# Weight pieces from one planned list, source order in the feed-forwards, and transposes of both token tiles

## The chip, the core and the metric

The kernel runs on one core of a Trainium2 chip. The metric is device time in microseconds (us) of one execution; the median of several runs counts, less is better.

## The reference

One decoder layer on 256 tokens of width 2048, all in float32:

```
x = x + 0.5 * swiglu(rmsnorm(x, w1), ffn1)        # gate, up: 2048 x 5632, down: 5632 x 2048
x = x + mixer(rmsnorm(x, w2))                     # w_in: 2048 x 8208, w_out: 2048 x 2048
x = x + 0.5 * swiglu(rmsnorm(x, w3), ffn2)
out = rmsnorm(x, w4)
swiglu(x) = (silu(x @ w_gate) * (x @ w_up)) @ w_down
```

The mixer has 8 heads of retention (rotary positions, fixed decays, a row norm and a gate) and 8 heads of a gated delta rule (a causal convolution over 4 tokens, l2 norms, decays computed from the input, a triangular solve in each chunk, a row norm and a gate). Both read one product with w_in, and one product with w_out takes both.

## The kernel before, in words

**Products.** Tokens stand in NT = 2 tiles of 128. Every weight is read once, in pieces of two row tiles by 512 columns, 512 KB each. A piece is loaded (`raw`, issued by SP, L126) and split exactly in two parts: ScalarE casts it to the high part (`whi`, L130), VectorE subtracts that from it for the low part (`wlo`, L131). The left operand has two parts as well (`xh` and `xl`, or `hh` and `hl`). `triple` (L139) adds three matmuls of 128x128 by 128x512: high by high (L144), high by low (L145), low by high (L146). A unit is one `triple`; a piece is four units, 12 matmuls, and serves both token tiles. `raw`, `whi` and `wlo` have four buffers each, so the cast of piece n + 4 waits until TensorE is done with piece n, and the load of piece n + 4 until VectorE has made `wlo` of piece n.

**Feed-forward** (`ffn`, L278). The 5632 inner columns are 11 blocks of 512, done in two halves of 6 and 5 blocks. A block is the product with w_gate, its silu on ScalarE (`sg`, L311), the product with w_up, and `h` on VectorE (L315): 192 matmuls in 16 pieces. `h` has tokens in the partitions and must become a left operand: VectorE transposes it in squares of 32x32 (`vector_transposed`, L217). One operation takes 32 partitions of one token tile into one quadrant of 32 partitions of `ht`, 32x128 elements; 32 of them make a block. Then ScalarE copies `ht` to `hh` (L136) and VectorE makes `hl` (L137), in two halves. This work is not issued at once: it goes as small functions into the list `later`, and `product` (L207) takes one of them after every second unit of the next product. After a half's blocks come four column blocks of the product with w_down, added to x by VectorE (L331). In the second half of the first feed-forward, x's new columns are transposed and scaled for the mixer's norm in the same way (`norm_block`, L250). The last column block of the last product runs one token tile after the other at its end (`staggered_product`, L174).

**Start.** The first block of the first feed-forward alternates between the two products, two contraction tiles at a time. `start` (L347) loads x transposed, scales it for the first norm (`norm_tile`, L231, on ScalarE and VectorE), loads x itself and sums its squares on ScalarE.

**Mixer** (L423). 16 products with w_in run as units; after each unit, chains of stages (generators) are advanced: convolution, delta rule, retention, rotary angles, and the transposes of the heads' outputs (`mixed_chain`, L830). A stage yields the number of units to wait for. In the delta rule the rows of a matrix go to DRAM and come back broadcast over 32 partitions (`nr`, L721, issued by POOL), and VectorE uses them in `yn` (L736). Two loads of retention's decays (`rd`, L877) are issued from ScalarE's queue.

**What sets the order.** The kernel is written in a framework that follows dependences and buffers by itself. Its scheduler plays the program through with modelled durations and gives each engine a fixed list of instructions: among those that are ready by its model, the one that stands first in the source. Each engine then works through its list in that order, and each instruction waits until what it needs is really there. So an instruction can stand ahead of another one because the model thought that it would be ready sooner.

Of the kernel before, what the change touches and what calls it, by code (L numbers as in the profile page):

```python
# [29 lines left out]
Q = 32           # partitions of a quadrant  # L30
KEPT = 4         # weight pieces of the last product that stay on chip
NLEV = 7         # log2 of the delta-rule chunk (128)
# [11 lines left out]
# columns of the constant table  # L44
# [10 lines left out]
def _constants():  # L55
    """Masks, identity, rotary frequencies and retention decays: functions of shapes alone."""
# [27 lines left out]
def hybrid_layer(ctx: ExitStack, tc: tile.TileContext, a: dict, out: bass.AP):  # L84
    nc = tc.nc
    V, S, G, PE = nc.vector, nc.scalar, nc.gpsimd, nc.tensor

# [12 lines left out]
    # the norms' weights; x transposed follows them  # L100
# [10 lines left out]
    # the tensor engine's clock rises only under load: it starts while the first loads are on their way  # L111
# [6 lines left out]
    # the left operand of every product, as contraction tiles in two parts  # L118
# [4 lines left out]
    def weight_piece(src, k, n, pool=wsp, both=None):  # L123
        """both: where the parts go, instead of tiles of the pool."""
        raw = wraw.tile([P, k, n], F32, name="raw")
        nc.sync.dma_start(raw, src)  # L126
        if both is None:
            both = pool.tile([P, k, n], F32R, name="whi"), pool.tile([P, k, n], F32R, name="wlo")
        hi, lo = both
        S.copy(hi, raw)  # L130
        V.tensor_tensor(lo, raw, hi.bitcast(F32), ALU.subtract)  # L131
        return hi, lo

    def split(hi, lo, src):
# [13 lines left out]
    def product_pieces(rows, w, c0, sizes=()):  # L148
        """The row tiles of w[:, c0:c0+NB] in pieces: (positions in rows, source)."""
# [6 lines left out]

    def product_units(left, w, rows, c0, sizes=()):
        """PSUM accumulators, one per token tile, of left.T @ w[rows, c0:c0+NB], and a generator that fills them.

        left(k): the two parts of contraction tile k, [128, T] each;  # L160
        rows: pairs (k, row tile of w), in order."""
        accs = [acc.tile([P, NB], F32, name="acc") for _ in range(NT)]

        def units():
            for ks, src in product_pieces(rows, w, c0, sizes):
                hi, lo = weight_piece(src, len(ks), NB)
                for j, k in enumerate(ks):
                    for t in range(NT):
                        triple(accs[t], left, rows[k][0], t, hi[:, j, :], lo[:, j, :], k == 0, k == len(rows) - 1)
                        yield  # L170
# [3 lines left out]
    def staggered_product(left, w, rows, c0, pool, kept):  # L174
        """The same product, one token tile after the other at its end; yields an accumulator when it is full.
        The last `kept` pieces of the weight stay in pool."""
# [4 lines left out]
        def piece(i, t):  # L181
            if t == 0:
                ks, src = pieces[i]
                split_pieces[i] = weight_piece(src, len(ks), NB, pool if i >= len(pieces) - kept else wsp)
# [4 lines left out]
        lag = 2  # L189
        for i in range(len(pieces)):  # L190
# [10 lines left out]
    later = deque()      # work whose inputs are on their way: done bit by bit beside the next product  # L201
# [63 lines left out]
    def power(dst, src, e, w):  # L265
        """src ** e, element by element, on a small tile."""
# [11 lines left out]
    def ffn(idx, factor, after, lead=None):  # L278
        """factor(): the row factors; after(b, t, pool): follows the sum of column block b and token tile t;
        lead(k, pool): makes contraction tiles k and k + 1 of the left operand."""  # L280
# [5 lines left out]
        with (tc.tile_pool(name=f"ffn{idx}", bufs=1) as hp, tc.tile_pool(name=f"ffe{idx}", bufs=1) as ep,  # L286
              tc.tile_pool(name=f"wlast{idx}", bufs=KEPT) as wl):
            hh = hp.tile([P, len(halves[0]) * kb, T], F32R, name="hh")
# [5 lines left out]
            for hf in halves:  # L294
                rows = [(k, k) for k in range(KD)]
                for i, b in enumerate(hf):
                    u = None
                    if b == 0 and lead:
                        g, gs = product_units(x_left, wg, rows, 0, (1, 1))
                        u, us = product_units(x_left, wu, rows, 0)  # L300
                        for k in range(0, KD, 2):
                            lead(k, ep)
                            for units in (gs, us):
                                deque(islice(units, 2 * NT), 0)
                    else:
# [18 lines left out]
                for b in range(nout):  # L324
                    if last and idx == 2 and b == nout - 1:
                        o = staggered_product(h_left, wd, rows, b * NB, wl, KEPT)
# [20 lines left out]
    def start(k, pool):  # L347
        """Contraction tiles k and k + 1 from the transposed x; x itself comes along, a column block behind."""
# [28 lines left out]
    ffn(1, lambda: row_factor(ssqs[0]), to_mixer, start)  # L377

# [44 lines left out]
def mixer(tc, a, gd, env):  # L423
# [7 lines left out]
    GH = 4                       # heads of a group  # L431
# [3 lines left out]
    with ExitStack() as ctx:  # L435
# [61 lines left out]
        def gates_chain():  # L497
# [5 lines left out]
            # the weight's two parts side by side as the left operand: their products are added at the end  # L503
# [39 lines left out]
            # exp of sums of g: from the chunk's start to a token, and from a token to the end of chunk 0  # L543
# [8 lines left out]
        def rotary_chain():  # L552
# [15 lines left out]
            # whole turns off, coarsely (any size of position), then the nearest one;  # L568
            # turns and 2 pi in parts whose products are exact
# [38 lines left out]
        def tokens(src, c):  # L608
            """Chunk c of src [channel, 4, tokens] -> PSUM [token, 4, channel]."""
# [22 lines left out]
        def delta_chain(gi, kq, vT):  # L632
            """The delta rule of a group of heads; gates[gi] becomes its gated output."""
            hs = gi * GH
            kT, qT = kq[:, :, 0, :], kq[:, :, 1, :]
            # decays exp(sum of g over (s, t]) of each head and chunk, [s, t], zero for t < s
# [14 lines left out]
            # k and q back to tokens for their norms; k of chunk 0, decayed to the chunk's end  # L651
# [24 lines left out]
            # scores with decay, [s, t]: N.T (its diagonal is never read) and the attention's  # L676
# [13 lines left out]
            # X = (I + N)^-1 and Y = X.T  # L690
# [5 lines left out]
            def quad(f, m=P):  # L696
                """Four narrow products, each beside one of the running product's units, which hide its operand's load."""
# [7 lines left out]
            # blocks of the diagonal of N.T, [row, matrix, column in block], by way of DRAM to all rows of their block  # L705
# [19 lines left out]
            # column j of the inverse's transpose times row j of N.T leaves the columns to the right  # L725
# [18 lines left out]
            # then by doubling the blocks: only the left half of the columns of a doubled block of X changes  # L744
# [26 lines left out]
            # the two chunks  # L771
# [19 lines left out]
            # row norm, with q's own factor in it  # L791
# [57 lines left out]
        def rotated_chain(src, dst):  # L849
            """src [tokens, t, 4*128] -> rotary -> dst [d, 4, tokens]."""  # L850
# [23 lines left out]
        def retention_chain(hs, qT, kT, v, gate):  # L874
            """Retention of a group of heads; the gates, when they come, become its gated output."""
# [123 lines left out]
```

## Time and profile before

Three runs took 2058.64, 2060.18 and 2061.57 us, median 2060.18. The profiled execution has a span of 2058.5 us between its first and last instruction.

| engine | busy us | share of the span | instructions |
|---|---|---|---|
| TensorE, matmuls (PE) | 1995.6 | 97% | 8804 |
| TensorE, weight loads (PEld) | 1617.5 | 79% | 8804 |
| VectorE (DVE) | 1400.9 | 68% | 2390 |
| ScalarE (ACT) | 896.8 | 44% | 1076 |
| GpSimd (POOL) | 89.4 | 4% | 121 |

8160 of the 8804 matmuls are the wide ones of the products. Matmuls are pipelined: one is shown as some 0.39 us long while the next one has started, so a high busy share doesn't say that TensorE is as fast as it can be. The distance between the starts of two matmuls says that. The memory moved 379.94 MB, 185 GB/s over the span; the mean granted clock of TensorE is 0.992 of full speed.

### The profile page before, as it was taken

The numbers are of one execution on the slowest core, as the hardware profiler recorded it, in microseconds if no ns is written. First come the engines' busy times: TensorE is split into PE (matmuls) and PEld (weight loads), VectorE is DVE, ScalarE is ACT, GpSimd is POOL, SyncE is SP. The second block draws the span as 40 slices with busy tenths as digits, with TensorE's granted clock in tenths as the row PEclk, the third lists the DMA queues.
The fourth block names the chain that finished last, engine by engine and source line by source line (L and its number), as shares of the span: only waits on it lengthen the run. The fifth ranks groups of instructions, "written<-read, shape, count | busy, mean of one in ns | idle before, by whom it ended". The sixth has DMA issues, their size and how long they took to land.

```text
span 2058.5 us, 24232 instructions
## 1 busy us (share of the span) xinstructions
PE 1995.6 (97%) x8804; PEld 1617.5 (79%) x8804; DVE 1400.9 (68%) x2390; ACT 896.8 (44%) x1076; POOL 89.4 (4%) x121
## 2 busy tenths in 40 slices
PE   9999999999999999988998989999999999999998
PEld 7777878887787778876877778788887888887786
DVE  6777764457776866564897698866677544677754
ACT  6444443344444446633643334444444434444443
POOL 0000000000000000320132100000000000000000
PEclk9999999999999999999999999999999999999999
DMA  8555655565565565697468545665555656655564
GB/s 302 188 166 184 197 195 189 190 187 171 184 196 196 169 202 174 146 205 172 136 182 190 132 133 195 205 189 188 187 183 173 209 194 192 190 187 164 185 214 143
DMA packets 197608, 379.94 MB, mean 185 GB/s; under 512 B 15280, under 2 KB 15920, under 8 KB 197360
## 3 DMA queue, kind: packets, MB, share of 16 engines
q1 hardware_dynamic: 193600, 367.35, 58.3%
q0 software_dynamic: 3168, 8.65, 1.6%
q10 hardware_dynamic: 720, 2.38, 0.3%
q8 instruction: 69, 1.13, 0.2%
q14 instruction: 51, 0.42, 0.1%
HBM read 375.98 MB, written 2.36 MB: 184 GB/s over the span
## 4 chain that ended last, share of the span: by engine, by line
PE 69%; DVE 22%; DMA 3%; issue 3%; ACT 2%; POOL 1%; SPq 0%; DVEq 0%; POOLq 0%; ACTq 0%
PE acc L145 22%; PE acc L146 22%; PE acc L144 22%; DVE ht L222 10%; DVE wlo L131 7%; ACT whi L130 2%; DVE h L315 1%; DMA nr<-nd 1%; DVE mt L222 1%; DMA raw<-in_w_in_dram 1%; DVE y L222 1%; PE mx L702 1%; PE mx L624 0%; DMA x<-in_x_dram 0%; PE mx L683 0%
## 5 line engine op out<-in xcount | busy, mean ns | idle before, releaser
L131 DVE TENSOR_TENSOR wlo<-raw,whi 128x1024 fp32r<-128x1024 f32 (+1 forms) x689 | 838.0, 1224 | 537.9 <-ACT whi L130 532.9
L130 ACT CAST whi<-raw 128x1024 fp32r<-128x1024 f32 (+1 forms) x689 | 722.7, 1051 | 934.3 <-PE acc L146 750.8
L145 PE MATMUL acc<-wlo,xh 128*128 128x512 f32 x1920 | 757.2, 394 | 27.1 <-DVE wlo L131 25.4
L144 PE MATMUL acc<-whi,xh 128*128 128x512 f32 x1920 | 760.7, 397 | 0.1
L146 PE MATMUL acc<-whi,xl 128*128 128x512 f32 x1920 | 752.9, 392 | 0.0
L145 PEld LDWEIGHTS acc<-wlo,xh 128*128 128x128 f32 x1920 | 362.9, 189 | 117.5 <-DVE wlo L131 46.9
L146 PEld LDWEIGHTS acc<-whi,xl 128*128 128x128 f32 x1920 | 362.9, 189 | 74.6
L144 PEld LDWEIGHTS acc<-whi,xh 128*128 128x128 f32 x1920 | 362.8, 189 | 74.5 <-ACT whi L130 1.2
L145 PE MATMUL acc<-wlo,hh 128*128 128x512 f32 x704 | 277.6, 394 | 5.0 <-DVE wlo L131 4.8
L144 PE MATMUL acc<-whi,hh 128*128 128x512 f32 x704 | 276.5, 393 | 0.0
L146 PE MATMUL acc<-whi,hl 128*128 128x512 f32 x704 | 276.5, 393 | 0.0
L222 DVE STREAM_TRANSPOSE ht<-h 32x128 f32<-32x128 f32 x704 | 213.0, 302 | 10.1
L145 PEld LDWEIGHTS acc<-wlo,hh 128*128 128x128 f32 x704 | 132.3, 188 | 38.7 <-DVE wlo L131 9.3
L144 PEld LDWEIGHTS acc<-whi,hh 128*128 128x128 f32 x704 | 132.4, 188 | 30.0
L146 PEld LDWEIGHTS acc<-whi,hl 128*128 128x128 f32 x704 | 132.4, 188 | 29.4
L136 ACT CAST hh<-ht 128x512 fp32r<-128x512 f32 x44 | 25.1, 619 | 89.9 <-DVE ht L222 89.9
L267 POOL TENSOR_TENSOR rfac<-rms,cexpn 128x2 f32<-128x2 f32 (+1 forms) x5 | 4.3, 863 | 875.4 <-DVE rms L273 836.4
L145 PE MATMUL acc<-wlo,mh 128*128 128x512 f32 x96 | 38.6, 402 | 3.0 <-DVE wlo L131 3.0
L146 PE MATMUL acc<-whi,ml 128*128 128x512 f32 x96 | 38.0, 396 | 0.0
L144 PE MATMUL acc<-whi,mh 128*128 128x512 f32 x96 | 38.0, 396 | 0.0
L736 DVE TENSOR_TENSOR yn<-nr,Yd 128x248 f32<-128x248 f32 (+30 forms) x62 | 19.0, 307 | 24.4 <-DMA nr<-nd 23.0
L713 POOL MEMSET Y<- 128x1024 f32 x2 | 1.9, 968 | 767.5 <-PE acc L146 714.9
(205 smaller groups left out, 915.8 us busy)
## 6 DMA issues: line engine op xcount, KB each, us to landing
raw<-in_ffn_w_up_dram SPq DMA_DIRECT2D x176, 512.0 KB, 4.5
raw<-in_ffn_w_down_dram SPq DMA_DIRECT2D x176, 512.0 KB, 4.4
raw<-in_ffn_w_gate_dram SPq DMA_DIRECT2D x175, 512.0 KB, 4.3
raw<-in_w_in_dram SPq DMA_DIRECT2D x128, 512.0 KB, 4.9
raw<-in_w_out_dram SPq DMA_DIRECT2D x32, 512.0 KB, 3.8
nr<-nd POOLq DMA_DIRECT2D x64, 128.0 KB, 7.1
x<-in_x_dram SPq DMA_DIRECT2D x4, 512.0 KB, 7.1
out_dram<-x SPq DMA_DIRECT2D x8, 256.0 KB, 2.4
```

The lines of the kernel that those rows point to most:

```text
L130: S.copy(hi, raw)
L131: V.tensor_tensor(lo, raw, hi.bitcast(F32), ALU.subtract)
L136: S.copy(hi, src)
L144: PE.matmul(o, lhsT=sh, rhs=hi, start=first, stop=False)
L145: PE.matmul(o, lhsT=sh, rhs=lo, start=False, stop=False)
L146: PE.matmul(o, lhsT=sl, rhs=hi, start=False, stop=last)
L222: V.transpose(dst[q:q + Q, :, t * P + r:t * P + r + Q], src[r:r + Q, t, :].rearrange("p (n c) -> p n c", c=P)[:, :, q:q + Q])
L267: G.tensor_tensor(dst, src, cexp[e][:, 0:1].broadcast_to([P, w]), ALU.pow)
L315: V.scalar_tensor_tensor(h[:, t, :], u[t], rf[:, t:t + 1], sg[:, t, :], ALU.mult, ALU.mult)
L702: PE.matmul(pt[:m, i, :], lhsT=lhsT, rhs=rhs, start=True, stop=True)
L713: G.memset(Y, 0.0)
L736: V.tensor_tensor(yn[:, :, :w], nr[:, j - j0, :, j + 1:], Yd[:, :, j:j + 1].broadcast_to([P, NM, w]), ALU.mult)
```

## The change

Four things are different.

1. One list (`Stream.plan`) is filled before the work begins, with every weight piece of the products in the order of use. `take` hands out the next piece, and before that issues the load and the split of the pieces up to `lead` further on. `lead` is 0 for the first two contraction tiles, 1 in the rest of the first block and in the last staggered product, and 3 elsewhere.
2. In both feed-forwards TensorE, VectorE and ScalarE issue their instructions in the order of the source (`tc.manual_schedule`). Instructions from outside the feed-forwards may still be put among them by the scheduler, and the loads on SP stay its own.
3. `vector_transposed` takes both token tiles in one operation, 32x256 elements, so that 16 make a block; the lists in `later` and the stages of `mixed_chain` that do them are half as many.
4. Smaller moves: in `start` the squares of a column block of x are summed when the next one's tiles begin, the last ones in `first_factor`; the load of retention's decays goes from ScalarE's queue to SP's; the order of the output projection's rows is a constant; comments are gone.

```
+    class Stream:
+        def __init__(self):
+            self.plan, self.ready, self.at, self.lead = [], deque(), 0, 0
+        def add(self, w, pieces, pool=None):
+            self.plan += [(w, src, len(ks), pool) for ks, src in pieces]
+        def take(self, w, n):
+            while self.at < len(self.plan) and len(self.ready) <= self.lead:
+                name, src, k, pool = self.plan[self.at]
+                self.ready.append((name, k, weight_piece(src, k, NB, pools[pool] if pool else wsp)))
+                self.at += 1
+            name, k, parts = self.ready.popleft()
+            assert (name, k) == (w, n)
+            return parts
...
         def units():
-            for ks, src in product_pieces(rows, w, c0, sizes):
-                hi, lo = weight_piece(src, len(ks), NB)
+            for ks, _ in product_pieces(rows, w, c0, sizes):
+                hi, lo = stream.take((w.tensor.name, c0), len(ks))
...
     def vector_transposed(dst, src):
-        def piece(t, r):
+        dv = dst.rearrange("p n (t c) -> p t n c", t=NT)
+        sv = src.rearrange("p t (n c) -> p t n c", c=P)
+        def piece(r):
             for q in range(0, P, Q):
-                V.transpose(dst[q:q + Q, :, t * P + r:t * P + r + Q],
-                            src[r:r + Q, t, :].rearrange("p (n c) -> p n c", c=P)[:, :, q:q + Q])
-        return [partial(piece, t, r) for t in range(NT) for r in range(0, P, Q)]
+                V.transpose(dv[q:q + Q, :, :, r:r + Q], sv[r:r + Q, :, :, q:q + Q])
+        return [partial(piece, r) for r in range(0, P, Q)]
...
-        with (tc.tile_pool(name=f"ffn{idx}", bufs=1) as hp, tc.tile_pool(name=f"ffe{idx}", bufs=1) as ep,
+        with (tc.manual_schedule(engines={E.PE, E.DVE, E.Activation}), tc.tile_pool(name=f"ffn{idx}", bufs=1) as hp, tc.tile_pool(name=f"ffe{idx}", bufs=1) as ep,
...
                             for units in (gs, us):
                                 deque(islice(units, 2 * NT), 0)
+                            stream.lead = 1
+                        stream.lead = LEAD
...
+    ffn_plan(1, True)
+    mixer_plan()
+    ffn_plan(2, False)
...
         if r:
             cs = slice(b * NB, (b + 1) * NB)
             nc.sync.dma_start(x[:, :, cs], xv[:, :, cs])
-            for t in range(NT):
-                square_sum(ssqs[0], b, t)
+        elif b:
+            for t in range(NT):
+                square_sum(ssqs[0], b - 1, t)
...
-            nc.scalar.dma_start(rd.rearrange("p h t -> p (h t)"), a["cst"][:, C_DEC + hs * T:C_DEC + (hs + GH) * T])
+            nc.sync.dma_start(rd.rearrange("p h t -> p (h t)"), a["cst"][:, C_DEC + hs * T:C_DEC + (hs + GH) * T])
```

## Rows read from the trace of the kernel before

**Rows 1.** Windows (start:end): length, busy us and instructions by engine, clock, DMA share, GB/s.

```profile
4.97:754.81 749.84, 737.01 (x3168) 594.68 (x3169) 513.69 (x839) 327.11 (x371) 0.74 (x1) 1.00 0.60 194
4.97:279.11 274.14, 267.89 (x1153) 216.78 (x1154) 195.69 (x333) 129.59 (x157) 0.74 (x1) 1.00 0.64 209
754.81:1217.78 462.97, 437.20 (x2074) 356.66 (x2072) 325.49 (x665) 213.52 (x312) 85.55 (x113) 0.97 0.67 166
1217.78:1312.45 94.67, 91.69 (x385) 71.64 (x384) 83.11 (x172) 41.33 (x55) 0.00 (x0) 1.00 0.53 178
1312.45:2049.25 736.80, 725.93 (x3176) 593.30 (x3175) 474.87 (x705) 311.26 (x333) 2.31 (x2) 1.00 0.58 189
1583.72:1715.75 132.03, 131.15 (x578) 107.95 (x576) 74.27 (x91) 51.68 (x50) 0.00 (x0) 1.00 0.58 191
1939.21:2049.25 110.04, 109.16 (x480) 89.75 (x479) 66.74 (x91) 45.55 (x54) 0.55 (x1) 1.00 0.51 173
```

**Rows 2.** Timeline, TensorE: start, duration, instruction, [idle before, releaser].

```profile
144.07 0.39 PE L144 MATMUL acc<-whi,xh 128*128 128x512 f32 x1
...
152.23 0.39 PE L144 MATMUL acc<-whi,xh 128*128 128x512 f32 x1
152.72 0.50 PE L145 MATMUL acc<-wlo,xh 128*128 128x512 f32 x1
...
155.38 0.39 PE L144 MATMUL acc<-whi,xh 128*128 128x512 f32 x1
156.52 0.50 PE L145 MATMUL acc<-wlo,xh 128*128 128x512 f32 x1 [0.74 <-DVE wlo L131]
...
160.07 0.39 PE L145 MATMUL acc<-wlo,xh 128*128 128x512 f32 x1
...
170.72 0.39 PE L144 MATMUL acc<-whi,xh 128*128 128x512 f32 x1
...
189.08 0.39 PE L144 MATMUL acc<-whi,xh 128*128 128x512 f32 x1
...
301.01 0.40 PE L146 MATMUL acc<-whi,hl 128*128 128x512 f32 x1
...
310.85 0.40 PE L146 MATMUL acc<-whi,hl 128*128 128x512 f32 x1
```

**Rows 3.** Timeline, VectorE, at the same block's start (x: instructions in a row).

```profile
145.10 6.30 DVE L222 STREAM_TRANSPOSE ht<-h 32x128 f32<-32x128 f32 x20
151.44 1.23 DVE L131 TENSOR_TENSOR wlo<-raw,whi 128x1024 fp32r<-128x1024 f32 x1
```

**Rows 4.** Timeline, ScalarE, at the same block's start.

```profile
144.27 1.06 ACT L130 CAST whi<-raw 128x1024 fp32r<-128x1024 f32 x1 [1.67 <-PE acc L146]
...
157.79 1.15 ACT L136 CAST hh<-ht 128x512 fp32r<-128x512 f32 x2 [4.31 <-DVE ht L222]
```

**Rows 5.** Groups by form, VectorE: count | busy us, mean ns | idle before.

```profile
L222 DVE STREAM_TRANSPOSE ht<-h 32x128 f32<-32x128 f32 x704 | 213.0, 302 | 10.1
...
L743 DVE STREAM_TRANSPOSE X<-Y 128x512 f32<-128x512 f32 x4 | 2.6, 690 | 1.5 <-POOL Y L740 1.5
```

**Rows 6.** Timeline, ScalarE, start of the program.

```profile
4.06 0.62 ACT L130 CAST whi<-raw 128x512 fp32r<-128x512 f32 x1 [1.40 <-DMA raw<-in_ffn_w_gate_dram]
...
5.51 0.50 ACT L237 ACTIVATE xh<-h,nwt 128x256 fp32r<-128x256 f32 x1
```

**Rows 7.** Waits of TensorE, 50 to 70 us: total us, times, longest.

```profile
PE acc L145 <- DVE wlo L131: 2.4, 4, 0.8
```

**Rows 8.** Waits of TensorE, then VectorE, 850 to 1260 us.

```profile
PE acc L145 <- DVE wlo L131: 9.9, 5, 6.2
PE mx L702 <- DVE X L743: 9.4, 2, 5.6
...
DVE yn L736 <- DMA nr<-nd: 23.0, 7, 12.0
```

**Rows 9.** DMA issues: queue, count, KB each, median us to landing.

```profile
rd<-in_cst_dram ACTq DMA_DIRECT2D x2, 512.0 KB, 7.1
```

More of the change, by code (lines that the diff above doesn't have):

```diff
@@ L31 @@
 KEPT = 4
+LEAD = 3
 NLEV = 7
@@ L42 @@
 N_IN = 8 * RET_W + 2 * NH
+OUT_ORDER = [(4 * i + j, r0 + j) for i, r0 in enumerate((NH, NH + 4, 0, 4)) for j in range(4)]
 C_ID = 0
@@ L86, in hybrid_layer @@
     V, S, G, PE = nc.vector, nc.scalar, nc.gpsimd, nc.tensor
+    E = mybir.EngineType
     const = ctx.enter_context(tc.tile_pool(name="const", bufs=1))
@@ L155, in product_pieces, with whole @@
             k += n
+    class Stream:
[11 more added lines that the diff above has]
+            return parts
+    stream, pools = Stream(), {}
+    def whole(w, rows, c0, sizes=()):
+        stream.add((w.tensor.name, c0), product_pieces(rows, w, c0, sizes))
     def product_units(left, w, rows, c0, sizes=()):
@@ L172, in product_units, with staggered_product @@
         return accs, units()
-    def staggered_product(left, w, rows, c0, pool, kept):
+    def staggered_product(left, w, rows, c0, kept):
         accs = [acc.tile([P, NB], F32, name="acc") for _ in range(NT)]
@@ L182, in piece @@
             if t == 0:
-                ks, src = pieces[i]
-                split_pieces[i] = weight_piece(src, len(ks), NB, pool if i >= len(pieces) - kept else wsp)
+                split_pieces[i] = stream.take((w.tensor.name, c0), len(pieces[i][0]))
             hi, lo = split_pieces[i]
@@ L285, in ffn @@
         rf = None
-        with (tc.tile_pool(name=f"ffn{idx}", bufs=1) as hp, tc.tile_pool(name=f"ffe{idx}", bufs=1) as ep,
+        with (tc.manual_schedule(engines={E.PE, E.DVE, E.Activation}), tc.tile_pool(name=f"ffn{idx}", bufs=1) as hp, tc.tile_pool(name=f"ffe{idx}", bufs=1) as ep,
               tc.tile_pool(name=f"wlast{idx}", bufs=KEPT) as wl):
+            pools["last"] = wl
             hh = hp.tile([P, len(halves[0]) * kb, T], F32R, name="hh")
@@ L304, in ffn @@
                                 deque(islice(units, 2 * NT), 0)
+                            stream.lead = 1
+                        stream.lead = LEAD
                     else:
@@ L325, in ffn @@
                     if last and idx == 2 and b == nout - 1:
-                        o = staggered_product(h_left, wd, rows, b * NB, wl, KEPT)
+                        o = staggered_product(h_left, wd, rows, b * NB, KEPT)
                     else:
@@ L333, in ffn, with rows_of, ffn_plan, mixer_plan @@
                             after(b, t, ep)
+    def rows_of(k0, n):
+        return [(k, k0 + k) for k in range(n)]
+    def ffn_plan(idx, lead):
+        wg, wu, wd = a[f"ffn{idx}_w_gate"][0], a[f"ffn{idx}_w_up"][0], a[f"ffn{idx}_w_down"][0]
+        nblk, nout, kb = FF // NB, D // NB, NB // P
+        halves = [range(0, (nblk + 1) // 2), range((nblk + 1) // 2, nblk)]
+        for hf in halves:
+            for b in hf:
+                if b == 0 and lead:
+                    g = list(product_pieces(rows_of(0, KD), wg, 0, (1, 1)))
+                    u = list(product_pieces(rows_of(0, KD), wu, 0))
+                    gn, un = (wg.tensor.name, 0), (wu.tensor.name, 0)
+                    stream.add(gn, g[:1])
+                    g = g[1:]
+                    for i in range(len(u)):
+                        stream.add(gn, g[i:i + 1])
+                        stream.add(un, u[i:i + 1])
+                else:
+                    whole(wg, rows_of(0, KD), b * NB)
+                    whole(wu, rows_of(0, KD), b * NB)
+            rows = rows_of(hf[0] * kb, len(hf) * kb)
+            for b in range(nout):
+                if idx == 2 and hf is halves[1] and b == nout - 1:
+                    pieces = list(product_pieces(rows, wd, b * NB))
+                    stream.add((wd.tensor.name, b * NB), pieces[:-KEPT])
+                    stream.add((wd.tensor.name, b * NB), pieces[-KEPT:], "last")
+                else:
+                    whole(wd, rows, b * NB)
+    def mixer_plan():
+        wi, wo = a["w_in"][0], a["w_out"][0]
+        half = RET_W // 2
+        for c0 in ([O_GK, O_GQ, O_GV, O_GZ, O_GZ + half] + [o + half for o in (O_GK, O_GQ, O_GV)]
+                   + [o + g for g in (0, half) for o in (O_RQ, O_RK, O_RV, O_RG)]):
+            whole(wi, rows_of(0, KD), c0)
+        pair = [list(product_pieces(OUT_ORDER, wo, b * NB)) for b in range(2)]
+        first = 3 * len(pair[0]) // 4
+        for part in (slice(0, first), slice(first, None)):
+            for b in range(2):
+                stream.add((wo.tensor.name, b * NB), pair[b][part])
+        for b in range(2, D // NB):
+            whole(wo, OUT_ORDER, b * NB)
+    ffn_plan(1, True)
+    mixer_plan()
+    ffn_plan(2, False)
     ssqs = [small.tile([P, NT, D // NB], F32, name=f"ssq{i}", bufs=1) for i in range(4)]
@@ L375, in to_mixer, with first_factor @@
             later.extend(norm_block(ssqs[1], 1, b, None if b == D // NB - 1 else pool.tile([P, NB // P, T], F32, name="ht")))
-    ffn(1, lambda: row_factor(ssqs[0]), to_mixer, start)
+    def first_factor():
+        for t in range(NT):
+            square_sum(ssqs[0], D // NB - 1, t)
+        return row_factor(ssqs[0])
+    ffn(1, first_factor, to_mixer, start)
     with tc.tile_pool(name="gd", bufs=1) as gd:
@@ L951, in mixer @@
         chains.append(mixed_chain(GH, r1, ["vh", "ml"]))
-        order = [(4 * i + j, r0 + j) for i, r0 in enumerate((NH, NH + GH, 0, GH)) for j in range(4)]
         def m_left(k):
             return tuple(p[:, k % 4, :] for p in mixed[k // 4][1:])
-        pair = [product_units(m_left, a["w_out"][0], order, b * NB) for b in range(2)]
+        pair = [product_units(m_left, a["w_out"][0], OUT_ORDER, b * NB) for b in range(2)]
         for _, units in pair:
@@ L966, in mixer @@
         for b in range(2, D // NB):
-            o = product(m_left, a["w_out"][0], order, b * NB)
+            o = product(m_left, a["w_out"][0], OUT_ORDER, b * NB)
             last = b == D // NB - 1
```

## The prediction

> **What bounds the kernel now.** I read the stage table first: busy time and matmul counts over stretches cut where the left operand of the products changes. The first feed-forward issues 3168 wide matmuls in 749.84 us, the second the same number in 736.80 us, the output projection 384 in 94.67 us, and the mixer's products with their small matmuls take 462.97 us [rows 1]. TensorE is busy nearly all the time in every stage but the mixer, so the question is how fast it could go. The timeline of TensorE answers: undisturbed, matmuls start 0.2267 us apart (47 of them from 160.07 to 170.72); in another stretch they start 0.2343 us apart (42 from 301.01 to 310.85) [rows 2]. The first figure is my floor, since the granted clock is 1.00 in both feed-forwards [rows 1] and nothing in the change makes a matmul shorter. Against it, 3168 x 0.2267 = 718.1 us, the first feed-forward loses 31.7 us and the second 18.7; 384 x 0.2267 = 87.0, so the output projection loses 7.6. Together 58.0 us that are not arithmetic.
>
> Where they go is seen at a block boundary. The L145 matmul at 152.72 comes 0.49 us after its predecessor and the one at 156.52 comes 1.14 us after, idle until VectorE's wlo. From one block's first matmul (144.07) to the next one's (189.08) it is 45.01 us for 192 matmuls, 43.53 at the floor: 1.5 us a block [rows 2]. There are 11 blocks in each feed-forward, so 22 x 1.5 = 33 us of the 58. VectorE's own timeline gives the reason: after h it runs 20 transposes in a row (6.30 us from 145.10) and only then, at 151.44, the wlo whose whi ScalarE had finished at 145.33 [rows 3, 4]. The work fits (VectorE is busy 514 of 750 us [rows 1]); its order doesn't. The slower pace of 0.2343 makes most of the rest: it follows such stalls, and where the first down product holds it through, it costs 576 x 0.0076 = 4.4 us.
>
> **The change, part by part.** *Transposes of both token tiles.* An operation of 128 elements takes 302 ns, one of 512 takes 690 [rows 5]: 1.01 ns an element over a fixed 173. For 256 elements that gives 431 ns; with the gap that 20 in 6.30 us show, 315 - 302 = 13 ns, a pitch of 0.444 us. A block has 16 of them instead of 32: 7.1 us against 10.1. It can't be under 0.315 (the half-size one's pitch); from above I take the 512-element row with its gap, 0.70. I choose 0.444, on the line between both; the pattern has one more dimension than either row, which is the doubt. Off the path by itself: VectorE has idle time, so the 3 us count only through the order.
> [...]
>
> *Source order, three pieces ahead.* I place one block by hand, time 0 being the next product's first matmul (144.07). h is over when the transposes start, at 1.0; whi of piece 3 ends at 1.26 [rows 2 to 4]; its wlo follows at once and ends at 2.55 (1.23 and a gap [rows 3]). Behind it the source has, on VectorE, four transposes, wlo 4, eight transposes, wlo 5, four transposes: 16p + 2.5, so with pitch p they end at 5.05 + 16p. Now the one place where source order hurts: on ScalarE the cast of piece 6 stands behind the copy hh, and hh waits for the last transpose. hh 0.64 (half of 1.15, and a gap), cast 1.06 [rows 4], wlo 1.25: wlo 6 ends at 8.0 + 16p. TensorE wants it six pieces of 12 matmuls, plus one, later: 16.55. With p = 0.444 it ends at 15.1, so 1.4 us are left; wlo 3, 4 and 5 (2.55, 5.6, 10.4) have over 3 us each. No stall; and with no stall, no slow pace after it. The lead as such gives nothing here: today's casts already wait for TensorE to free one of four buffers (1.67 us at 144.27 [rows 4]), which is a lead of three. What is late next after a block is nothing until p reaches 0.534.
> Other waits that source order fixes: the gate's activation waits for the product's end on ScalarE with one cast behind it, which waits for the same end (its buffer), and then has 8 us; x-updates and norm tiles in the down products are the same burst with 1.4 + 7.1 us and fit likewise. SP's weight loads stay with the scheduler and follow wlo, up to four pieces ahead of it.
>
> *Start.* On ScalarE the scaling of contraction tile 1 now stands before the first casts (0.62 at 4.06; the scaling ran at 5.51 for 0.50 [rows 6]). The first cast is later by at least that 0.50 and at most 1.95, if the scaling can't start before 5.51. I take 1.0. At the first block boundary the lead grows from one to three pieces behind h. Before, four waits idled TensorE there for 2.4 us [rows 7]; I leave half, since the mixer's rotary angles may still be put among VectorE's work at this place.
>
> *Mixer.* Its own order stays the scheduler's. Its losses are of another kind: TensorE idle 9.9 us for wlo and 9.4 for X, VectorE 23.0 idle in front of yn for the broadcast loads nr [rows 8]; the wlo stand behind the blocked yn. A lead of three doesn't move yn. The decay load (two of 512 KB [rows 9]) moves from ScalarE's queue to SP's, ahead of weight loads that have up to four pieces of cover (48 matmuls, 11 us); if it waits longer for its buffer, TensorE waits for the rest. Twelve microseconds, the spread of such shifts (half of the 23.0), is my bound to either side; I take 0, as rows show losses that the edit doesn't touch. The output projection has the same bursts as a block, in the scheduler's order but with half the operations: of 7.6 I leave 3.
>
> *Sum.* The cleanest down products show what is left without slow pace: 132.03 - 576 x 0.2267 = 1.5 and 110.04 - 480 x 0.2267 = 1.2 [rows 1]. I leave 1.3 for each of the eight stages of the two feed-forwards, 10.4. The first of them loses 274.14 - 1152 x 0.2267 = 13.0 today [rows 1]; less 4 boundaries x 1.5 that is 7.0 for the start and the first boundary, of which I leave 7.0 - 1.2 + 1.0 = 6.8. Kept: 10.4 + 6.8 + 3.0 = 20.2. Gained: 58.0 - 20.2 = 37.8. The profiled execution spans 2058.5 us, 1.7 under the median of the timed runs; 2058.5 - 37.8 + 1.7 = 2022.4, so 2022.
>
> **The rivals.** *A: the transposes cost twice as much.* If the merged pattern gets no benefit from one instruction (p = 0.63), wlo 6 ends at 18.1, 1.5 late in each block: the stall is today's, at piece 6 instead of pieces 3 and 4. Left is the 1.2 us at the first boundary: 2059, no change to speak of. For it: the new pattern is in no row. Against: both rows lie on one line.
> *B: slower, by the same chain.* From p = 0.63 each further 0.1 us costs 16 x 0.1 = 1.6 us a block, because hh holds ScalarE's casts in source order, where the scheduler could put them ahead. At 0.70, the 512-element row with its gap, 2.7 a block instead of 1.5: 22 x 1.2 = 26 us more: 2086. It decides at p = 0.63. For it: nothing but the missing row. Against: half as many elements as the row it needs.
> *C: the mixer slips.* The scheduler plans wlo, yn and the small products anew; one more blocked yn like the first (12 of the 23.0 us) with its half-clock matmuls costs up to 15 us, two 28. 2037 to 2050. For it: the mixer's granted clock of 0.97 and idle 19 us show how plan and loads already disagree [rows 1, 8]. Against: the same units and stages, less VectorE work.
> *D: order was not it.* If the scheduler's order in the feed-forward already equals the source order up to the burst, halved transposes alone do the work: 10 in a row, 4.4 us, would let wlo 3 end at 6.7 against 8.4. Same time as my forecast, other cause.
>
> **How the numbers follow.** Forecast (with D) 0.63, its own range 2010 to 2034 (12 us of mixer to each side); better than 2010: 0.07, the mixer gaining; C 0.15; A 0.07; B 0.05; anything else slower 0.03. Faster 0.85 (forecast, better, C). A run can't tell less than 0.2%, 4 us, from no change: A is there, 0.07. Slower 0.08. The range 2005 to 2050 leaves out A, B and little at the bottom.
>
> **What would show it.** Right: mean of the merged transpose near 431 ns; no idle before L145 in the feed-forwards; the starts 0.2267 apart in the first down products; feed-forwards near 730 and 723 us (718.1 plus what is kept). Wrong: idle before L145 at piece 6 of each block behind ScalarE's hh (A, B); feed-forwards as forecast but the mixer far from 463 us (C); blocks still losing 1.5 us in spite of short transposes, which no case above holds.

## The result, and the profile after

The changed kernel takes 2015.02 us (median of 4 runs, 2013.94 to 2015.32) against 2060.88 for the kernel before on the same chip: ratio 0.9775, 95% interval 0.9763 to 0.9787. The forecast was 2022, own range 2010 to 2034.

The span of the profiled execution falls from 2058.5 to 2013.5 us, by 45.0. The page first, its line of engines.

```profile
PE 1974.1 (98%) x8804; PEld 1617.5 (80%) x8804; DVE 1315.8 (65%) x1878; ACT 890.9 (44%) x1076; POOL 86.9 (4%) x121
```

TensorE has as many matmuls as before, and VectorE 512 instructions less (1878 for 2390). Next the stage table of the changed kernel, cut as in [rows 1] with the same columns: first feed-forward, its first down product, mixer, output projection, second feed-forward, its first down product.

```profile
6.22:735.20 728.98, 727.34 (x3169) 595.16 (x3169) 476.18 (x613) 323.67 (x370) 0.71 (x1) 1.00 0.61 200
...
270.17:405.11 134.94, 134.94 (x578) 108.49 (x577) 71.82 (x75) 51.34 (x50) 0.00 (x0) 1.00 0.56 187
735.20:1195.48 460.28, 434.20 (x2074) 353.70 (x2072) 318.20 (x619) 213.48 (x312) 84.16 (x113) 0.97 0.68 165
1195.48:1285.44 89.96, 89.96 (x386) 72.32 (x384) 76.88 (x119) 43.89 (x60) 0.00 (x0) 1.00 0.56 187
1285.44:2004.26 718.82, 718.82 (x3177) 595.13 (x3175) 439.90 (x516) 305.87 (x328) 1.24 (x2) 1.00 0.59 193
1547.49:1678.05 130.56, 130.56 (x577) 108.11 (x576) 71.64 (x75) 51.47 (x50) 0.00 (x0) 1.00 0.58 193
```

Against [rows 1], the first feed-forward gives 20.86 us, the second 17.98, the output projection 4.71, the mixer 2.69; the first wide matmul starts 1.25 later (6.22 for 4.97). That is the whole 45.0, up to rounding. Above the floor of 0.2267 us a matmul the first feed-forward now loses 10.9 us, the output projection 2.9, the second feed-forward 0.7. The two down products have 576 matmuls each: 130.56 is 0.2267 apiece, 134.94 is 0.2343. Neither is ever idle, and yet one is 4.4 us longer.

The block that the prediction placed by hand starts at 139.60 in this trace (144.07 before). TensorE's timeline (start, duration, instruction) shows no idle time in it, not at piece 6 (156.15) either, and the next block follows after 43.52 us for 45.01 before [rows 2]:

```profile
139.60 0.39 PE L149 MATMUL acc<-whi,xh 128*128 128x512 f32 x1
...
156.15 0.39 PE L150 MATMUL acc<-wlo,xh 128*128 128x512 f32 x1
...
183.12 0.39 PE L149 MATMUL acc<-whi,xh 128*128 128x512 f32 x1
```

VectorE's timeline of the same stretch (x: instructions in a row; in brackets the idle time before) has, in place of 20 transposes in a row [rows 3], groups of four and eight with wlo between them:

```profile
140.89 1.23 DVE L136 TENSOR_TENSOR wlo<-raw,whi 128x1024 fp32r<-128x1024 f32 x1 [0.17 <-ACT whi L135]
142.03 1.78 DVE L254 STREAM_TRANSPOSE ht<-h 32x256 f32<-32x256 f32 x4
143.84 1.23 DVE L136 TENSOR_TENSOR wlo<-raw,whi 128x1024 fp32r<-128x1024 f32 x1
145.10 3.58 DVE L254 STREAM_TRANSPOSE ht<-h 32x256 f32<-32x256 f32 x8
148.71 1.23 DVE L136 TENSOR_TENSOR wlo<-raw,whi 128x1024 fp32r<-128x1024 f32 x1
149.97 1.79 DVE L254 STREAM_TRANSPOSE ht<-h 32x256 f32<-32x256 f32 x4
152.45 0.69 DVE L142 TENSOR_TENSOR hl<-ht,hh 128x512 fp32r<-128x512 f32 x1 [0.69 <-ACT hh L141]
153.40 1.22 DVE L136 TENSOR_TENSOR wlo<-raw,whi 128x1024 fp32r<-128x1024 f32 x1 [0.26 <-ACT whi L135]
```

And ScalarE's, with the copy hh that waits for the last transpose and the cast of piece 6 behind it (before: [rows 4]):

```profile
151.79 0.62 ACT L141 CAST hh<-ht 128x512 fp32r<-128x512 f32 x1 [5.50 <-DVE ht L254]
152.32 1.05 ACT L135 CAST whi<-raw 128x1024 fp32r<-128x1024 f32 x1
```

The merged transpose, in the groups by form (count, busy us, mean ns, idle before); the half-size one had 302 ns and the 512-element one 690 [rows 5]:

```profile
L254 DVE STREAM_TRANSPOSE ht<-h 32x256 f32<-32x256 f32 x352 | 153.3, 436 | 5.3
```

The start, on TensorE and ScalarE: the scaling now runs ahead of the first casts, which begin at 5.57 for 4.06 [rows 6].

```profile
6.22 0.49 PE L149 MATMUL acc<-whi,xh 128*128 128x512 f32 x1 [1.35 <-DVE xl L269]
...
5.15 0.51 ACT L268 ACTIVATE xh<-h,nwt 128x256 fp32r<-128x256 f32 x1 [2.49 <-DMA h<-in_xt_dram]
5.57 2.07 ACT L135 CAST whi<-raw 128x512 fp32r<-128x512 f32 x3
```

### The profile page after: what moved, and what is told of

Read it like the earlier page. It is cut to its first block, busy times and chain, and to the rows that moved or that the text cites. A ratio compares the mean times of both kernels' runs of the same rounds, so it can differ in the third digit from the quotient of the medians.

```text
span 2013.5 us, 23688 instructions
## 1 busy us (share of the span) xinstructions
PE 1974.1 (98%) x8804; PEld 1617.5 (80%) x8804; DVE 1315.8 (65%) x1878; ACT 890.9 (44%) x1076; POOL 86.9 (4%) x121
## 4 chain that ended last, share of the span: by engine, by line
PE 85%; DVE 5%; DMA 4%; issue 4%; POOL 1%; ACT 1%; DVEq 0%; POOLq 0%; ACTq 0%
PE acc L149 28%; PE acc L151 27%; PE acc L150 27%; DMA nr<-nd 2%; DVE wlo L136 2%; DMA raw<-in_w_in_dram 1%; PE mx L791 1%; DVE mt L254 0%; PE mx L713 0%; DMA nd<-Nd 0%; DVE yn L825 0%; ACT whi L135 0%; DVE Yd L826 0%; POOL nr L810 0%; DVE ht L254 0%
## 5 line engine op out<-in xcount | busy, mean ns | idle before, releaser
L254 DVE STREAM_TRANSPOSE ht<-h 32x256 f32<-32x256 f32 x352 | 153.3, 436 | 5.3
L142 DVE TENSOR_TENSOR hl<-ht,hh 128x512 fp32r<-128x512 f32 x44 | 30.3, 688 | 14.5 <-ACT hh L141 14.4
L345 ACT ACTIVATE sg<-acc,rfac 128x512 f32<-128x512 f32 x44 | 29.9, 689 | 20.2 <-PE acc L151 17.4
```

The lines of the kernel that those rows point to most:

```text
L254: V.transpose(dv[q:q + Q, :, :, r:r + Q], sv[r:r + Q, :, :, q:q + Q])
L345: S.activation(sg[:, t, :], g[t], AF.Silu, scale=rf[:, t:t + 1])
```

## The experiments

Times are medians; ratios are to the kernel before, run beside. Each edit is against the changed kernel, except where it says the kernel before.

**e1, short transposes alone.** The kernel before, with only `vector_transposed` as in the change:

```
-        def piece(t, r):
+        def piece(r):
...
+                V.transpose(dv[q:q + Q, :, :, r:r + Q], sv[r:r + Q, :, :, q:q + Q])
```

> The kernel before with the merged transposes alone. In its planned order all 16 stand in a row between h and the wlo of piece 3. At the 0.436 us they took in the changed kernel and a gap they end 8.3 us after the block's first matmul, wlo 3 at 9.55 against the 8.4 at which TensorE wants it: 1.2 us lost a block where it was 1.5. If the order decides (my theory): about 2055 us. If fewer transposes alone do it (rival D of the prediction): about 2018 us.

Measured 2053.0 us (2050.87 to 2057.99), ratio 0.9959 (0.9945 to 0.9974). VectorE's timeline, and the one matmul of TensorE's that idles in the same block:

```profile
145.22 7.18 DVE L225 STREAM_TRANSPOSE ht<-h 32x256 f32<-32x256 f32 x16
152.43 1.23 DVE L131 TENSOR_TENSOR wlo<-raw,whi 128x1024 fp32r<-128x1024 f32 x1
...
153.71 0.50 PE L145 MATMUL acc<-wlo,xh 128*128 128x512 f32 x1 [1.10 <-DVE wlo L131]
```

All 16 transposes stand ahead of the next wlo, 7.18 us where 20 of the old ones took 6.30: with the work halved the burst in front of wlo is no shorter. The five blocks of the first feed-forward's second half still lose 5.6 us (223.24 - 960 x 0.2267; 6.1 before). Order decides. The span is 7.9 us shorter all the same: 4.9 of it in the mixer (463.0 to 458.0), 2.5 in the second feed-forward.

**e2, the scheduler's order; e3, the list alone.** e2 takes out source order; e3 takes it out and has the old transposes as well, so that list, lead and the smaller moves are what is left of the change (e3's edit of `vector_transposed` is shown at e12).

```
-        with (tc.manual_schedule(engines={E.PE, E.DVE, E.Activation}), tc.tile_pool(name=f"ffn{idx}", bufs=1) as hp, ...
+        with (tc.tile_pool(name=f"ffn{idx}", bufs=1) as hp, ...
```

> The changed kernel with the feed-forwards' order left to the scheduler; list, lead of three and merged transposes stay. In its planned order the wlo stand between groups of at most 7 transposes: wlo 3 would end at 2.9 us, wlo 4 at 5.9, wlo 5 at 10.3, all before they are wanted (8.4, 11.1, 13.8). If the lead in the list is enough, no stall at a block and about 2015 us. If the fixed source order is what counts, the blocks lose 1.5 us again: about 2048 us.

> The list and the lead of three alone: the old transposes (32 a block) and the scheduler's order in the feed-forwards. In the planned order at most 9 transposes stand between two wlo; with 0.315 us each, wlo 3 to 7 end at 2.7, 6.5, 10.2, 14.3 and 17.4 us, wanted at 8.4, 11.1, 13.8, 16.5 and 19.3. If the lead does it: no stall, feed-forwards as in the changed kernel, about 2018 us with some loss left in the output projection. If the lead gives nothing, as the prediction says of it, or if the short transposes are needed: 2048 to 2060 us.

e2: 2013.27 us (2012.56 to 2014.57), ratio 0.9764 (0.9750 to 0.9779). e3: 2021.06 (2020.21 to 2021.65), 0.9801 (0.9786 to 0.9815). The first feed-forward, the output projection and the second feed-forward, in windows of e2:

```profile
4.83:734.60 729.77, 729.09 (x3170) 596.87 (x3169) 476.43 (x615) 326.87 (x371) 0.75 (x1) 1.00 0.62 200
1192.97:1282.93 89.96, 89.96 (x385) 72.32 (x384) 76.04 (x118) 43.89 (x60) 0.00 (x0) 1.00 0.54 182
1282.93:2001.72 718.79, 718.79 (x3177) 595.19 (x3175) 439.48 (x516) 307.54 (x328) 1.25 (x2) 1.00 0.60 193
```

and of e3:

```profile
4.81:733.74 728.93, 728.67 (x3169) 596.82 (x3169) 511.73 (x839) 326.43 (x371) 0.74 (x1) 1.00 0.62 200
1192.77:1288.81 96.04, 92.05 (x385) 71.64 (x384) 86.16 (x180) 43.45 (x58) 0.00 (x0) 1.00 0.52 176
1288.81:2009.46 720.65, 719.45 (x3176) 595.01 (x3175) 473.43 (x705) 310.28 (x333) 2.31 (x2) 1.00 0.60 193
```

Without source order and short transposes the feed-forwards are down to 728.9 and 720.7 us, within 2 us of the changed kernel. VectorE's timeline in e3, at the block that starts there at about 138, shows how: old transposes, the scheduler's order, and yet they come in groups of at most nine with a wlo after each, two of eight here.

```profile
140.69 2.51 DVE L251 STREAM_TRANSPOSE ht<-h 32x128 f32<-32x128 f32 x8
143.24 1.23 DVE L136 TENSOR_TENSOR wlo<-raw,whi 128x1024 fp32r<-128x1024 f32 x1
144.49 2.54 DVE L251 STREAM_TRANSPOSE ht<-h 32x128 f32<-32x128 f32 x8
```

The list issues a piece's split earlier in the source, ahead of transposes that stood before it. That changes its place in VectorE's list: the smaller moves touch the start and the mixer and not these blocks, and e1, which has neither list nor lead, has the burst. No run takes the lead back to none or one under the scheduler's order, so that it is the lead, and not the list by itself, rests on this reading of the order. Source order on top shows as no gain in time (the intervals of e2 and the changed kernel overlap); what the trace shows of it is the start, where the first wide matmul is at 4.83 without and at 6.22 with it.

**e4, a lead of one; e7, a lead of two.** One constant:

```
-LEAD = 3
+LEAD = 1        # e4; 2 in e7
```

> The changed kernel with a lead of one piece instead of three, source order kept. If order and buffers suffice, as the prediction says (the buffers alone are a lead of three): about 2015 us. If in source order the lead is the cover: in each block one stall of 1.0 us behind the silu (1.4 us of it, the cast 1.05 and wlo 1.25 against 2.95 us of cover) and two of 1.9 and 0.4 behind the transposes, 3.3 us for 22 blocks and less for the down products: about 2090 us.

> The changed kernel with a lead of two. By hand, in source order: wlo 4 ends at 10.3 us against 11.1, no stall; wlo 5 stands behind the last transposes and hh, ends at 15.0 against 13.9: one stall of 1.2 us in each of 22 blocks and a like one in the norm blocks, about 2043 us. If any lead above one is enough: 2015 us.

e4: 2130.4 us (2126.55 to 2131.06), ratio 1.0325 (1.0308 to 1.0342), slower than before. e7: 2038.06 (2037.93 to 2038.90), 0.9892 (0.9875 to 0.9908). In e4, TensorE's timeline has two waits for wlo behind the transposes. At the first, VectorE's list has eight transposes ahead of the wlo that TensorE wants; at the second, ScalarE's copy hh holds the cast of the piece (VectorE, ScalarE, TensorE):

```profile
152.94 3.58 DVE L254 STREAM_TRANSPOSE ht<-h 32x256 f32<-32x256 f32 x8
156.55 1.23 DVE L136 TENSOR_TENSOR wlo<-raw,whi 128x1024 fp32r<-128x1024 f32 x1
...
159.63 0.62 ACT L141 CAST hh<-ht 128x512 fp32r<-128x512 f32 x1 [10.50 <-DVE ht L254]
160.16 1.04 ACT L135 CAST whi<-raw 128x1024 fp32r<-128x1024 f32 x1
...
157.83 0.50 PE L150 MATMUL acc<-wlo,xh 128*128 128x512 f32 x1 [1.40 <-DVE wlo L136]
162.52 0.50 PE L150 MATMUL acc<-wlo,xh 128*128 128x512 f32 x1 [0.77 <-DVE wlo L136]
```

The blocks lose what the expectation counted (16.5 us more than in the changed kernel for the five of the first feed-forward's second half, 3.3 each), but the total is 40 us over its 2090: it had too little for the down products, which lose 33.7 us more in the profiles. In e7 one stall is left in the block, behind hh, and the time is 5 us under the expected 2043:

```profile
157.62 0.50 PE L150 MATMUL acc<-wlo,xh 128*128 128x512 f32 x1 [0.64 <-DVE wlo L136]
```

So in source order the lead is what pays for the transposes and hh in front of the splits, as the placing by hand had it: with three they are covered, with two a part sticks out, with one the order is worse than the one it replaced. The prediction's sentence that the lead gives nothing is wrong here too.

**e12, source order with the old transposes.** `vector_transposed` and its callers' lists as before:

```
-        def piece(r):
+        def piece(t, r):
...
-        return [partial(piece, r) for r in range(0, P, Q)]
+        return [partial(piece, t, r) for t in range(NT) for r in range(0, P, Q)]
```

> The changed kernel with the old transposes of one token tile: list, lead of three and source order kept. Each entry of the list of later work still holds four transposes, but there are eight entries instead of four, so the burst spreads over twice as many pieces. Theory (with a lead of three VectorE's list is early enough for either transpose): by hand the last transpose ends 17.6 us after the block's start, and the wlo behind the copy hh belongs to piece 8, wanted at 22.0 and ready at 20.6: no stall, the feed-forwards as in the changed kernel, only the output projection loses some 6 us more: 2021. Rival (the shorter transposes are what makes source order fit): the wlo behind hh is 1.5 us late in each of 22 blocks, 33 us: 2048 to 2054.

Measured 2022.85 us (2021.13 to 2023.79), ratio 0.9806 (0.9789 to 0.9822). Feed-forward, output projection, feed-forward:

```profile
6.27:735.55 729.28, 728.51 (x3169) 596.32 (x3170) 514.57 (x836) 322.09 (x370) 0.70 (x1) 1.00 0.61 199
1196.12:1291.98 95.86, 92.06 (x386) 71.63 (x384) 86.13 (x173) 43.13 (x55) 0.00 (x0) 1.00 0.52 176
1291.98:2012.21 720.23, 719.54 (x3176) 594.90 (x3175) 476.86 (x712) 306.89 (x336) 1.25 (x2) 1.00 0.59 193
```

The feed-forwards are again as in the changed kernel, to 0.3 and 1.4 us. The shorter transposes are worth their time in the output projection: 95.9 and 96.0 us without them (e12, e3), 90.0 with them (e2, the changed kernel). There e3 still has TensorE wait for wlo (total, times, longest), and the changed kernel has it busy for all of the 89.96 us:

```profile
PE acc L150 <- DVE wlo L136: 3.9, 7, 0.8
```

**e5, e6, e8, e9, e10, the slow pace.** The stages that run at 0.2343 have a left operand in other places of the on-chip memory than those at 0.2267. The trace shows no addresses; those used here were read from the built programs, in bytes within a partition. whi lies at 85152 in all kernels but e6, and its other buffers, wlo, and the low parts of the left operands are multiples of 1024 from their high parts, so one distance describes a stage. A tile without use in front of the left operands moves them; in the constants' pool (e6) it moves the weights as well.

```
+    pad = par.tile([P, 8], F32, name="pad")    # 32 bytes: e5, e8; 24 floats in e10, 40 in e9
+    nc.vector.memset(pad, 0.0)
...
+    pad = const.tile([P, 8], F32, name="pad")  # e6
+    V.memset(pad, 0.0)
```

e8, e9 and e10 leave out source order, as e2 does.

> The changed kernel with one unused tile of 32 bytes a partition, put in front of the left operands of the first feed-forward's down products and of the output projection. It moves them by 32 bytes in on-chip memory, to the offset within 64 bytes that the weight parts, xh, xl and the second feed-forward's left operands have. If the slow pace of 0.234 us, which these three stages hold without any stall, comes from where the operands lie: 0.2267 there, 4.4 + 3.7 + 2.9 = 11 us less, about 2004 us. If it comes from something else (what the prediction said: stalls): 2015 us.

> The changed kernel with the unused 32 bytes in front of nearly everything: weights, xh, xl and both feed-forwards' left operands move together, and so does the mixer's memory. If the slow pace comes from left operand and weights having different offsets within 64 bytes, each stage keeps its pace: 2015 us. If it comes from a left operand that starts at a multiple of 64 bytes, the gate, up and w_in products (5760 matmuls) and the second feed-forward's down products (1056) become slow and the three slow stages fast: 51 - 11 = 40 us more, 2055 us. If placement doesn't matter: 2015 us, but then the run before shows no gain.

> What the runs point to: list, lead of three and merged transposes with the scheduler's order, and the 32 bytes in front of the left operands. If both act: 2013 - 11 = 2002 us, the fastest so far. If the shift does nothing: 2013 us.

> The kernel of e8 with 160 unused bytes instead of 32, so that the left operands of the three slow stages stand as far from the weight parts, within 1024 bytes, as those of the second feed-forward do, which never lost anything. If the distance sets the pace: no excess over 0.2267 in the three stages, 8.3 us under e8, about 2004 us. If the 32 bytes of e8 already gave what there is: 2012 us.

> The same with 96 bytes. Between no shift (7.6 ns lost a matmul) and 32 bytes (5.7 ns) a straight line would give 1.9 ns at 96, 0.2286 us a matmul in the three stages; a step would give 5.7 or nothing.

The first down product of the first feed-forward (576 matmuls), then one further stage where shown. e5:

```profile
270.13:404.00 133.87, 133.87 (x578) 108.51 (x576) 71.79 (x75) 51.22 (x50) 0.00 (x0) 1.00 0.57 189
```

e6:

```profile
271.07:406.01 134.94, 134.94 (x578) 108.50 (x577) 71.80 (x75) 51.34 (x50) 0.00 (x0) 1.00 0.57 187
```

e10:

```profile
269.14:400.98 131.84, 131.84 (x577) 108.18 (x576) 71.65 (x75) 51.21 (x50) 0.00 (x0) 1.00 0.57 192
```

e9, with the output projection:

```profile
268.87:399.43 130.56, 130.56 (x577) 108.11 (x576) 71.61 (x75) 51.59 (x50) 0.00 (x0) 1.00 0.59 193
...
1185.32:1272.63 87.31, 87.31 (x385) 72.00 (x384) 74.57 (x117) 43.31 (x60) 0.00 (x0) 1.00 0.56 186
```

| kernel | left operand minus whi, modulo 1024 | first down product, us | over the floor, ns a matmul | time, us | ratio (interval) |
|---|---|---|---|---|---|
| changed | 864 | 134.94 | 7.6 | 2015.02 | 0.9775 (0.9763 to 0.9787) |
| e6, both moved by 32 | 864 | 134.94 | 7.6 | 2015.16 | 0.9779 (0.9764 to 0.9794) |
| e5, left operand by 32 | 896 | 133.87 | 5.7 | 2013.58 | 0.9770 (0.9756 to 0.9785) |
| e8, the same, scheduler's order | 896 | 133.87 | 5.7 | 2011.92 | 0.9763 (0.9748 to 0.9777) |
| e10, by 96 | 960 | 131.84 | 2.2 | 2007.5, one run | |
| e9, by 160 | 0 | 130.56 | 0.0 | 2003.42 | 0.9712 (0.9696 to 0.9728) |

e6 tells that the place as such does nothing; the others that the distance does. The expectations of e5 and e8 (pace gone after 32 bytes) fell: a quarter of the loss went, too little to tell in the time of a run. e10 came near the straight line of its expectation (2.2 ns for 1.9), and the rest of the way came with e9. The second feed-forward, at a distance of 0 in all of these, was at the floor from the start; the distance of xh, 768, costs nothing either (192 matmuls in the 43.52 us of the block above), so the relation isn't a line over the whole kilobyte. Nor does it need the whole kilobyte: the left operand of the second token tile lies 512 bytes (128 tokens of four bytes) behind that of the first, and in the trace of the changed kernel both tiles' matmuls keep one pace (from start to start 234.2 to 234.4 ns for each of the three of a unit in the first down product, in either tile). So 352 costs there what 864 does, and 512 and 256 cost as little as 0 and 768: the second feed-forward's first down product (130.56 us) and that block at xh hold the floor in both tiles. e9 is the fastest version: list, lead of three, short transposes, the scheduler's order and 160 bytes.

**e11, the same 160 bytes in the kernel before.**

```
+    pad = par.tile([P, 40], F32, name="pad")
+    nc.vector.memset(pad, 0.0)
```

> The kernel before with nothing but the 160-byte tile, so that the first feed-forward's hh and hl and the output projection's operands move by 160 bytes. Theory (the slow pace comes from the distance between left operand and weight parts, with or without stalls): 576 + 480 matmuls of the first feed-forward's down products and 384 of the output projection get 7.6 ns shorter, 10.9 us: 2050; the first down product falls from 136.0 to about 131.6 us, while the blocks keep their losses. Rival (the prediction's: slow pace follows the stalls, and the stalls stay): no change, 2061, the down product stays at 136.

Measured 2055.32 us (2051.70 to 2058.75), ratio 0.9969 (0.9956 to 0.9981): between the two expectations. The two down products of the first feed-forward in the kernel before:

```profile
279.11:415.11 136.00, 135.27 (x578) 108.32 (x577) 74.37 (x91) 51.54 (x50) 0.00 (x0) 1.00 0.57 186
638.76:754.81 116.05, 113.57 (x481) 90.01 (x480) 97.11 (x191) 51.63 (x66) 0.00 (x0) 1.00 0.54 178
```

and in e11:

```profile
278.80:410.83 132.03, 131.15 (x578) 107.99 (x576) 74.25 (x91) 51.67 (x50) 0.00 (x0) 1.00 0.58 191
634.29:750.27 115.98, 111.21 (x482) 89.48 (x480) 95.58 (x189) 51.53 (x66) 0.00 (x0) 1.00 0.53 178
```

The first loses its slow pace (136.00 to 132.03) with its stall in place, so the pace doesn't follow stalls. The second is no shorter: its matmuls are faster (busy 111.21 us for 113.57), but TensorE then waits for wlo longer. The waits of TensorE in that stretch (total, times, longest), the kernel before:

```profile
PE acc L145 <- DVE wlo L131: 2.5, 4, 0.7
```

e11:

```profile
PE acc L145 <- DVE wlo L131: 4.7, 7, 1.1
```

There VectorE's burst sets the end, and the faster TensorE waits for it, 4.7 us for 2.5. The output projection, where bursts are left as well, gave 0.9 of its 2.9 us (94.67 to 93.81). The expectation had missed that: of 10.9 us the span got 5.3. In e9, without the bursts, the same bytes bring 9.9 us over e2 (2013.27 to 2003.42; the ratios to the kernel before go from 0.9764 to 0.9712).

## Why the prediction was right, and where it wasn't

The time, the transposes and the placing by hand came out; the step that said which part of the change does it did not.

*Transposes.* Right: 436 ns for 431 forecast.

*The block by hand.* Right to 0.1 us. From its start, wlo 3, 4 and 5 end at 2.52, 5.47 and 10.34 us (forecast 2.55, 5.6, 10.4), the last transpose at 12.16 (12.15), wlo 6 at 15.02 (15.1), wanted at 16.55. No stall, as forecast; e4 and e7 show the same chain where it fails. Rivals A and B needed a pitch of 0.63 and fell with the 436 ns.

*"The lead as such gives nothing here."* Wrong, and the main failure: this was the step that named the cause. The casts did wait for buffers (1.67 us in [rows 4]), which the prediction took for a lead of three. But the stall was in VectorE's list, and what moves wlo there is where the split stands in the source. List and lead, with the smaller moves but without source order and short transposes, bring 40.9 of the 45.9 us (e3). Credit went to source order, which by e2 brings no measurable time, and with a lead of one costs it (e4). The time came out in spite of this because the change has both, and the placing by hand has the lead of three in it; that the number was right says nothing for the step.

*Rival D.* Half right. The scheduler's order does reach the changed kernel's time (e2), but not through halved transposes: D counted 10 in a row, and e1 has 16. Its time was the forecast's and its chance counted with the forecast's, so the measured time could not part the two; e1, e2 and e3 do.

*"With no stall, no slow pace after it."* Wrong. The 0.2343 pace stays without a stall in 576 + 480 matmuls of the down products and 384 of the output projection, 10.9 us in the changed kernel (e9 takes all but 0.3 of it). Before, some 1040 of the 1056 matmuls of the first feed-forward's down products kept that pace too: without the gaps of late matmuls the two products lose 4.4 and 3.6 us, so 7.9 of its 31.7 us were not stalls. Of the 1.3 us left for each of eight stages, the first feed-forward had 5.2 and kept 8.0, all of it the pace, and the second had 5.2 and kept 0.7: hence 718.8 for 723.

*Start and first boundary.* Right in two sizes, 1.25 us for the later start (forecast 1.0) and one wait left at the boundary, 0.8 for 1.2, and wrong in the sum: of 6.8 us left for both, 4.1 were kept (263.95 - 1152 x 0.2267 = 2.8 in the stage, and the 1.25). That makes up for the pace, so that the 730 forecast for the first feed-forward against 729.0 (730.2 with the later start) agrees by luck. Some 1.6 us of what the start gained come from slower matmuls before: in the profile of the kernel before, eight matmuls of the start are 427 ns apart (7.01, 7.44, 7.87 and so on, to 10.00), and the trace's first record of the granted clock, at full speed, begins at 10.24 us; in this one it begins at 5.26, and the matmuls are 227 to 235 apart from the third on. The four matmuls ahead of the first wide one run from 1.52 to 4.88 there and to 4.87 here. Whether the later record belongs to the kernel or to the execution was not shown. TensorE's waits from 50 to 75 us (before: [rows 7]):

```profile
PE acc L150 <- DVE wlo L136: 0.8, 1, 0.8
```

*Mixer and output projection.* Forecast 0 with 12 to either side; 2.7 gained. It takes 457.9 to 463.0 us in every kernel run here but e4 (465.1): that is the whole spread of replanning. VectorE's wait for the broadcast loads is as in [rows 8] (850 to 1260 us):

```profile
DVE yn L825 <- DMA nr<-nd: 24.9, 6, 9.2
```

yn still waits for nr, no less than before, and the mixer isn't the 15 us longer that C needed: C did not come. The output projection kept 2.9 us for 3.0, though for another reason: no burst is left, and all of it is the pace. No run undoes the moved decay loads or the other smaller moves by themselves.

*The sum.* Forecast gain 37.8, measured 45.0 on the span. By stages the difference of 7.2 is 4.5 from the second feed-forward and 2.7 from the mixer; in the first feed-forward the two errors above cancel.

## What to carry to other kernels

When an engine's fixed list holds work that is needed soon behind work that isn't, try first to issue the needed work earlier in the source: that can be enough (e3: 40.9 of the 45.9 us), and an order forced by hand then needs a lead that covers whatever it puts in front (2015 us with a lead of three, 2130 with one). Look at the distance between starts of undisturbed matmuls stage by stage; two paces at one clock and one shape (here 0.2267 and 0.2343 us at 1.00) are a loss to be found apart from all waits. Take the waits away before the pace, or a part of the gain of the pace goes into longer waits (e11: the span got 5.3 of 10.9 us).

## What the runs showed of the hardware that was not expected

One and the same form of matmul (128x128 by 128x512) was issued every 226.7 or every 234.3 ns with the granted clock at 1.00 in both, by the distance in on-chip memory between its left operand and its weight parts. Modulo 1024 bytes and for the first token tile, 864 gave 7.6 ns more on average, 896 gave 5.7, 960 gave 2.2, and 0 and 768 gave none; at 864 (234.2 to 234.4 ns), 0 and 768 the second token tile, 512 bytes further, had the same pace. The weight load itself is as long at either pace (108.49 us for 577 and 108.11 for 576, 188 ns). What in the memory or in TensorE makes this wasn't settled, and no other distances were tried.
